# Query and key projections of the mLSTM heads: both halves of the input in one 512-column product, one bank per half unit

## The chip, the cores and the metric

The kernel runs on one core of a Trainium2 chip. The metric is device time in microseconds; the time of the kernel before is the median of three runs. The trace comes from one execution taken by the hardware profiler.

## The reference

Two layers of a hybrid decoder trunk on 256 tokens of width 1024. Each layer normalizes x, multiplies it by one input matrix whose columns are shared among three groups of heads (mLSTM, MoBA, NSA), lets each group mix the tokens, multiplies by an output matrix, and then runs a feed-forward block of width 4096. What the change touches is the mLSTM part of the input projection and the convolution behind it:

```python
h = rmsnorm(x, norm_mix[l])
proj = jnp.einsum('bsd,de->bse', h, w_in[l])
...
qk = jax.nn.silu(causal_conv(jnp.concatenate([m_q, m_k], axis=-1), conv_qk[l]))
...
y_m = mlstm(qk[..., :M_WIDTH], qk[..., M_WIDTH:], m_v, m_o, ...)
```

m_q and m_k are 512 columns each; causal_conv is a four-tap convolution along the tokens, each column with its own taps.

## The kernel before

All products are made with float32 operands split into two parts, a high one (the value cast to the fast format, `fp32r`) and a low one (the residue). A product of x and w is the sum of three: high x high, high x low, low x high. ScalarE casts each loaded weight piece (`raw`) to its high part (`hi`, in `highs`), VectorE subtracts to get the low part (`lo`, in `lows`), and six buffers hold each kind. The input, transposed, stands in one tile `H` of shape [128, 8, 2, 256]: for each of the eight blocks of 128 input columns, 256 tokens of the high part and beside them 256 tokens of the low part (`L.Hh`, `L.Hl`).

The input projection of a layer goes by the list `ORDER`: o1, o6, o2, o3, the compression products c0 and c1, q0, c2, c3, o4, q1, q2, q3, o5. The o groups are made by `project` with the tokens as output rows. The four q units are made by `project_t` with the projected columns as output rows: unit c2 covers 256 columns, as two halves c of 128, from two weight pieces of four blocks each. Before, both halves share one PSUM bank of the tag "acc", 2 x 256 columns; in each half and block the three products have 256 columns each and add into the same 256 columns.

PSUM has eight banks: "acc" is given two of them and "wk" six. Everything of the projections goes to "acc". A bank is given back by `free` when the step that reads it has been issued, and the next `new("acc", ...)` waits for that.

`conv` drains unit c2: one VectorE multiply with the row scales `RB` (line 1241) reads the whole bank into `cx`, behind three zero columns; then come the taps (a ScalarE multiply and three VectorE multiply-adds for each half), a tanh, and the write of `MQ`, which the mLSTM scores read (`mlstm`).

The order of instructions on each engine is fixed when the kernel is built. `Flow` (lines 145 to 279) runs all steps as generators with a rank, keeps an estimated clock of each engine from the costs in `Engine.cost`, and each time issues the operation that can start first; among operations of one engine that could start at about the same time the one with the lower rank goes first. `main` (the projections) has rank 100, the steps that prepare other operands have ranks from 2 up, and the casts and residues of weights (`highs`, `lows`) move ahead of these when their due time is near. On the chip each engine then works through its list in order and waits at the head of it.

Names in the trace: `acc` and `wk` are PSUM banks, `th`, `cx`, `cv` are buffers of SBUF, `P` holds attention scores after the exponential (ACT, `P<-wk,nmx`), `N` and `t` are the normalization and rotation of the attention heads, `KV` and `KC` belong to the compressed keys, `mr` to the mLSTM gates. All compute instructions carry the line of the helper, L137.

Of the kernel before, what the change touches and what calls it, by code (L numbers as in the profile page):

```python
# [11 lines left out]
ALU = mybir.AluOpType  # L12
# [3 lines left out]
S = 256  # L16
# [128 lines left out]
class Flow:  # L145
# [25 lines left out]
    def free(self, *tiles):  # L171
        for t in tiles:
            name = t.tensor.name
            self.places[self.owner.pop(name)].append(self.used.get(name, ("", 0.0))[1])
# [107 lines left out]
def body(ctx, tc, x, w_in, b_if, conv_qk, m_norm, moba_g, nsa_qg, nsa_kg, cmp_pe, cmp_w1, cmp_w2,  # L282
# [11 lines left out]
    done, free, add = flow.done, flow.free, flow.add  # L294
# [3 lines left out]
    mm, tr, act, copy = pe.matmul, pe.transpose, ac.activation, ac.copy  # L298
    tt, ts, stt = dv.tensor_tensor, dv.tensor_scalar, dv.scalar_tensor_tensor

    def new(tag, *shape, dt=F32):
        return New(tag, (128, *shape), dt)
# [89 lines left out]
    t = 0.0  # L392
    for l in range(DEPTH):
        for name in ORDER:
            if name[0] == "c":
                s = int(name[1])
# [83 lines left out]
    def weights():  # L480

        j = taken[0]
        taken[0] += 1
        yield f"lo {j}"
        if j >= SPLIT0:
            yield f"los {j}"
        _, kk, n = pieces[j]
        t = parts.pop(j)
        return tuple(a[:, :kk * n].rearrange("p (k n) -> p k n", k=kk) for a in t) + (t,)
# [80 lines left out]
    def project_t(l, c2):  # L570

        L = Ls[l]
        L.o[c2] = po = yield new("acc", 2, S)
        ws = []
        for c in range(2):
            for k in range(8):
                if len(ws) == k // 4:
                    ws.append((yield from weights()))
                wh, wl = (t[:, k % 4, c * 128:(c + 1) * 128] for t in ws[k // 4][:2])
                yield mm(po[:, c, :], wh, L.Hh[:, k, :], start=k == 0, stop=False)  # L580
                yield mm(po[:, c, :], wh, L.Hl[:, k, :], start=False, stop=False)
                yield mm(po[:, c, :], wl, L.Hh[:, k, :], start=False, stop=k == 7)
                if c and k % 4 == 3:
                    free(*ws[k // 4][2])
        done.add(f"q{c2}{l}")

    def compress(l, s):

# [128 lines left out]
    def main():  # L717
        for l in range(DEPTH):
            for name in ORDER:
                if name in ("c0", "c2"):  # L720
                    yield from compress(l, int(name[1]))
                elif name[0] == "c":
                    continue
                elif name[0] == "q":
                    yield from project_t(l, int(name[1]))
                else:
                    yield from project(l, name, GROUPS[name][1])
            yield from out_project(l)
            yield from feed_forward(l)
# [498 lines left out]
    def conv(l, c2):  # L1228
        L = Ls[l]
        yield f"RB{l}"  # L1230
        yield "V2"
        yield f"q{c2}{l}"
        if c2 == 0:
            L.MQt = yield new("MQ", 2048)
            L.MQ = L.MQt.rearrange("p (a b) -> p a b", a=8)
            done.add(f"MQ{l}")
        yield f"MQ{l}"
        xt = yield new("cx", 520)
        cx = xt.rearrange("p (a b) -> p a b", a=2)
        yield gp.memset(cx[:, :, 0:3], 0.0)  # L1240
        yield tt(cx[:, :, 3:259], L.o[c2], L.RB[:, None, :].to_broadcast([128, 2, S]), op=ALU.mult)
        free(L.o[c2])
        cv = yield new("cv", 2, 256)
        for c in range(2):
            w = lambda j: V[:, 32 + (l * 4 + j) * 8 + c2 * 2 + c:][:, 0:1]
            yield act(cv[:, c, :], cx[:, c, 0:256], AF.Copy, scale=w(0))
        for c in range(2):
            for j in range(1, 4):
                yield stt(cv[:, c, :], cx[:, c, j:j + 256], w(j), cv[:, c, :], op0=ALU.mult, op1=ALU.add)
        free(xt)  # L1250
        th = yield new("th", 2, 256)
        yield act(th, cv, AF.Tanh, scale=0.5)
        yield stt(L.MQ[:, 2 * c2:2 * c2 + 2, :], th, 1.0, cv, op0=ALU.add, op1=ALU.mult)
        free(th, cv)
        done.add(f"c{c2}{l}")
# [70 lines left out]
    for l in range(DEPTH):  # L1326
        gens = [after_mix(l, i, n) for i, n in tiles] + [after_ffn(l, i, n) for i, n in tiles]
        gens += [square_scales(l), scales(l), cmp_inputs(l)]
        gens += [nsa_heads(l, i) for i in range(2)] + [cmp_keys(l), gates(l)] + [moba_heads(l, i) for i in range(2)]
        gens += [attention(l, nsa), score(l, nsa), values(l), out_gates(l)] + [numerators(l, i) for i in range(2)]  # L1330
        gens += [mlstm(l)] + [conv(l, c) for c in range(4)] + [attention(l, moba), score(l, moba)]
        for g in gens:
            add(g, 2 + len(flow.procs))
# [36 lines left out]
```

## Time and profile before

| | us |
|---|---|
| median of three runs (641.97 to 692.95) | 642.06 |
| the profiled execution's own time | 641.33 |
| its span, first to last instruction | 639.5 |
| TensorE busy | 632.6 |
| VectorE busy | 444.3 |
| ScalarE busy | 367.1 |

The span is the stretch that the trace covers; the execution's own time is 1.8 us longer, and sums are made against that time. Matmuls are pipelined and their ends are modelled, so how fast TensorE gets on is read from the starts of two rows that follow each other. A row that ends in xN merges N instructions; its first number is the start of the first.

### The profile page before, as it was taken

The page shows a single profiled execution, that of the slowest core. Times are in us where ns is not written, and L with a number is a line of the kernel's source. Part 1 is how long each engine was busy: PE and PEld are TensorE (multiplying, and loading weights), DVE is VectorE, ACT ScalarE, POOL GpSimd, SP SyncE. Part 2 cuts the span into 40 slices and gives each one's busy share as a digit, 9 for nine tenths or more (in the row PEclk, how much of TensorE's full clock was granted, in tenths as well). Part 3 has the DMA queues.
Part 4 walks back from the last instruction along what each step waited for, and adds up shares of the span by engine and source line. Part 5 has one row for each costly group of instructions (what it writes and reads, how often), then busy time and mean ns, then how long its engine had stood idle before and what let it go on. Part 6 is the DMA issues. An engine that isn't in the chain of part 4 may idle for free.

```text
span 639.5 us, 10252 instructions
## 1 busy us (share of the span) xinstructions
PE 632.6 (99%) x3815; PEld 545.6 (85%) x3815; DVE 444.3 (69%) x823; ACT 367.1 (57%) x718; POOL 28.8 (4%) x50
## 2 busy tenths in 40 slices
PE   9999999999999999999999999999999999999997
PEld 8798898888888888888899979988888888888885
DVE  5769898679566565656583979987776565665661
ACT  6669875547364544545484985946645553545440
POOL 1110200100000000000010111001000000000000
PEclk9999999999999999999999999999999999999999
DMA  8787524448656465655546925144476656565711
GB/s 296 221 285 246 158 75 132 131 133 245 208 166 217 155 225 165 213 182 181 148 125 204 330 73 171 61 127 153 158 222 203 192 179 213 162 216 156 223 37 66
DMA packets 79090, 112.78 MB, mean 176 GB/s; under 512 B 4896, under 2 KB 61248, under 8 KB 79040
## 3 DMA queue, kind: packets, MB, share of 16 engines
q1 hardware_dynamic: 79008, 112.12, 55.5%
q8 instruction: 30, 0.49, 0.3%
q14 instruction: 20, 0.16, 0.1%
q10 hardware_dynamic: 32, 0.01, 0.0%
HBM read 111.06 MB, written 1.05 MB: 175 GB/s over the span
## 4 chain that ended last, share of the span: by engine, by line
PE 93%; DVE 2%; DMA 2%; ACT 1%; issue 0%; POOL 0%; DVEq 0%; POOLq 0%; ACTq 0%
PE wk L137 57%; PE acc L137 37%; DMA raw<-in_w_in 2%; DVE lo L137 1%; ACT hi L137 1%; DVE N L137 0%; POOL rs L137 0%; DVE t L137 0%; ACT P L137 0%; DVE dg L137 0%; ACT R L137 0%; DVE x L137 0%; ACT H L137 0%; DVE hss L137 0%; DVE nmx L137 0%
## 5 line engine op out<-in xcount | busy, mean ns | idle before, releaser
L137 DVE TENSOR_TENSOR lo<-raw,hi 128x1024 fp32r<-128x1024 f32 (+4 forms) x209 | 240.2, 1167 | 122.6 <-ACT hi L137 121.6
L137 ACT CAST hi<-raw 128x1024 fp32r<-128x1024 f32 (+3 forms) x207 | 205.7, 1014 | 133.5 <-PE wk L137 112.2
L137 PE MATMUL wk<-H,hi 128*128 128x512 f32 x512 | 128.0, 391 | 0.0
L137 PEld LDWEIGHTS wk<-H,hi 128*128 128x128 f32 x512 | 93.7, 188 | 17.9
L137 PE MATMUL acc<-hi,H 128*128 128x512 f32 (+3 forms) x368 | 100.1, 353 | 0.0
L137 PE MATMUL acc<-hi,P 128*128 128x512 f32 x240 | 79.2, 391 | 0.0
L137 PE MATMUL wk<-hi,P 128*128 128x512 f32 x240 | 78.7, 389 | 0.0
L137 PEld LDWEIGHTS wk<-H,lo 128*128 128x128 f32 x512 | 69.9, 190 | 5.0
L137 PE MATMUL wk<-H,lo 128*128 128x256 f32 x512 | 71.4, 282 | 0.0
L137 PEld LDWEIGHTS acc<-hi,H 128*128 128x128 f32 x368 | 63.9, 188 | 6.4 <-issue 0.4
L137 PE MATMUL acc<-lo,H 128*128 128x512 f32 (+3 forms) x184 | 65.2, 354 | 0.0
L137 PEld LDWEIGHTS wk<-hi,P 128*128 128x128 f32 x240 | 45.1, 188 | 9.3
L137 PEld LDWEIGHTS acc<-hi,P 128*128 128x128 f32 x240 | 45.2, 188 | 8.9
L137 PE MATMUL acc<-H,hi 128*128 128x256 f32 x256 | 51.3, 292 | 0.0
L137 PE MATMUL acc<-lo,P 128*128 128x512 f32 x120 | 47.0, 392 | 0.0
L137 PE MATMUL wk<-lo,P 128*128 128x512 f32 x120 | 46.7, 389 | 0.0
L137 ACT COPY th<-wk 128x256 f32<-128x256 f32 x64 | 23.9, 373 | 35.7 <-PE wk L137 35.7
L137 PEld LDWEIGHTS acc<-H,hi 128*128 128x128 f32 x256 | 40.4, 191 | 0.7 <-issue 0.5
L137 PEld LDWEIGHTS acc<-lo,H 128*128 128x128 f32 x184 | 34.6, 188 | 3.6 <-issue 0.7
L137 PE MATMUL acc<-H,lo 128*128 128x256 f32 x128 | 37.4, 292 | 0.1
L137 ACT ACTIVATE H<-wk,V 128x128 fp32r<-128x128 f32 x64 | 18.5, 373 | 22.7 <-PE wk L137 19.1
L137 DVE TENSOR_TENSOR cx<-wk,th 128x256 f32<-128x256 f32 x64 | 26.9, 421 | 2.2 <-ACT th L137 2.2
(199 smaller groups left out, 793.3 us busy)
## 6 DMA issues: line engine op xcount, KB each, us to landing
raw<-in_w_ff SPq DMA_DIRECT2D x128, 512.0 KB, 4.4
raw<-in_w_in SPq DMA_DIRECT2D x40, 512.0 KB, 5.1
raw<-in_w_out SPq DMA_DIRECT2D x16, 512.0 KB, 3.8
whole<-in_cmp_w SPq DMA_DIRECT2D x16, 256.0 KB, 4.8
raw<-in_w_in SPq DMA_DIRECT2D x8, 384.0 KB, 4.5
raw<-in_w_in SPq DMA_DIRECT2D x8, 268.0 KB, 3.5
raw<-in_w_in SPq DMA_DIRECT2D x8, 264.0 KB, 3.1
x<-in_x SPq DMA_DIRECT2D x4, 256.0 KB, 4.9
```

The costliest lines, as they stand in the source:

```text
L137: o = Op(self.name, lambda: f(out, *args, **kw), outs, ins, self.cost(op, outs, ins))
```

## The change

`project_t` now takes one bank of "acc" for each half of a unit. For each block the high weights multiply both parts of the input in one product of 512 columns, which leaves high x high in the bank's first 256 columns and high x low in the second 256. The low weights times the high input add 256 columns to the first half of the bank. Four wide products are followed by four narrow ones, for each of the two weight pieces. `conv` waits for each half by itself, copies the bank's second 256 columns to SBUF on ScalarE (into a `th` buffer), adds the first 256 columns on VectorE, and gives the bank back; the multiply with `RB` comes when both halves are in `cx`.

```diff
     def project_t(l, c2):
 
         L = Ls[l]
-        L.o[c2] = po = yield new("acc", 2, S)
         ws = []
+        g = dict(skip_group_check=True)
         for c in range(2):
-            for k in range(8):
-                if len(ws) == k // 4:
+            L.o[c2, c] = po = yield new("acc", 2, S)
+            for s in range(2):
+                if len(ws) == s:
                     ws.append((yield from weights()))
-                wh, wl = (t[:, k % 4, c * 128:(c + 1) * 128] for t in ws[k // 4][:2])
-                yield mm(po[:, c, :], wh, L.Hh[:, k, :], start=k == 0, stop=False)
-                yield mm(po[:, c, :], wh, L.Hl[:, k, :], start=False, stop=False)
-                yield mm(po[:, c, :], wl, L.Hh[:, k, :], start=False, stop=k == 7)
-                if c and k % 4 == 3:
-                    free(*ws[k // 4][2])
-        done.add(f"q{c2}{l}")
+                ks = range(s * 4, s * 4 + 4)
+                wh, wl = (t[:, :, c * 128:(c + 1) * 128] for t in ws[s][:2])
+                for k in ks:
+                    yield mm(po, wh[:, k % 4], L.H[:, k], start=k == 0, stop=k == 7, **g)
+                for k in ks:
+                    yield mm(po[:, 0, :], wl[:, k % 4], L.Hh[:, k, :], start=False, stop=k == 7, **g)
+                if c:
+                    free(*ws[s][2])
+            done.add(f"q{c2}{c}{l}")
...
-        yield f"q{c2}{l}"
+        yield f"q{c2}0{l}"
...
-        yield tt(cx[:, :, 3:259], L.o[c2], L.RB[:, None, :].to_broadcast([128, 2, S]), op=ALU.mult)
-        free(L.o[c2])
+        for c in range(2):
+            yield f"q{c2}{c}{l}"
+            o = L.o[c2, c]
+            t = yield new("th", 512)
+            yield copy(t[:, :S], o[:, 1, :])
+            yield tt(cx[:, c, 3:259], o[:, 0, :], t[:, :S], op=ALU.add)
+            free(o, t)
+        yield tt(cx[:, :, 3:259], cx[:, :, 3:259], L.RB[:, None, :].to_broadcast([128, 2, S]), op=ALU.mult)
```

The planner makes another order of it. The first place is TensorE in layer 0, where q0 ends and o4 begins. Before, acc_698 is q0's one bank and acc_883 is o4's; wk_681 is the compression, wk_900 the C,KV product.

```order
L137 MATMUL wk_849<-ident_79,cg_82 36x128 x2
L137 MATMUL acc_698<-H_70,hi_599 128x256 x2
L137 MATMUL acc_698<-H_70,lo_655 128x256
L137 MATMUL wk_681<-whole_699,MQ_439 32x128 x8
L137 MATMUL wk_681<-whole_715,MQ_439 32x128 x8
L137 MATMUL acc_883<-hi_641,H_70 128x512
L137 MATMUL acc_883<-lo_712,H_70 128x512
L137 MATMUL acc_883<-hi_641,H_70 128x512 x2
L137 MATMUL acc_883<-lo_712,H_70 128x512
L137 MATMUL wk_900<-C_85,KV_894 128x256
```

Now the same place, where acc_802 is the bank of q0's second half and acc_886, o4's, is the bank that q0's first half (acc_698) had.

```order
L137 MATMUL acc_802<-H_70,hi_599 128x512
L137 MATMUL acc_802<-H_70,lo_655 128x256 x4
L137 MATMUL wk_681<-whole_699,MQ_439 32x128 x8
L137 MATMUL wk_681<-whole_715,MQ_439 32x128 x8
L137 MATMUL wk_844<-ident_79,cg_82 36x128 x2
L137 MATMUL wk_873<-C_85,KV_862 128x256
L137 MATMUL acc_886<-hi_641,H_70 128x512
L137 MATMUL acc_886<-lo_712,H_70 128x512
```

The transposes of cg and the C,KV product now stand ahead of o4's first product, which takes a bank that q0 has just used. The second place is ScalarE's queue at the same time, in the new order; th_866 and th_885 are the copies of q0's two halves.

```order
L137 ACTIVATE P_799,sm01_771<-wk_752,nmx01_770 128x128
L137 ACTIVATE P_800,sm01_771<-wk_752,nmx01_770 128x128 x2
L137 ACTIVATE P_799,sm01_771<-wk_753,nmx01_770 128x128 x2
L137 COPY KV_862<-wk_681 128x128
L137 ACTIVATE P_800,sm01_771<-wk_753,nmx01_770 128x128 x2
L137 COPY th_866<-acc_698 128x256
L137 ACTIVATE KV_878<-wk_873 128x256
L137 COPY th_885<-acc_802 128x256
```

The copies stand behind the exponentials, and the reading of wk_873 stands between them. The third place is VectorE in layer 0, where q1 hands its first bank to q2. Before, q1's only read of its bank (acc_1095) stands here:

```order
L137 TENSOR_REDUCE nmx11_1235<-wk_1206 128x2
L137 TENSOR_REDUCE nmx11_1235<-wk_1207 128x2
L137 TENSOR_TENSOR Ml_72<-wk_897,Mh_71 128x2x128
L137 TENSOR_REDUCE nmx11_1235<-wk_1208 128x2
L137 TENSOR_REDUCE nmx11_1235<-wk_1209 128x2
L137 TENSOR_TENSOR cx_1257<-acc_1095,RB_97 128x2x256
L137 TENSOR_TENSOR lo_1215<-raw_996,hi_1198 128x1024
L137 TENSOR_TENSOR lo_1304<-raw_1051,hi_1258 128x1024
L137 RECIPROCAL sm11_1236<-sm11_1236 128x8
```

Now the bank of q1's first half is acc_1137, and its add is the last of these rows:

```order
L137 RECIPROCAL sm11_1088<-sm11_1088 128x8
L137 TENSOR_TENSOR N_1167<-R_708,hr81_1200 128x512
L137 TENSOR_TENSOR sm11_1088<-sm11_1088,GT1_102 128x4
L137 TENSOR_TENSOR N_1167<-N_1167,GB_91 128x256 x2
L137 TENSOR_SCALAR P_1151<-P_1151,sm11_1088 128x256
L137 TENSOR_TENSOR t11_728<-N_1167,C_85 128x128
L137 TENSOR_TENSOR t21_729<-N_1167,C_85 128x8x8 x2
L137 TENSOR_SCALAR P_1151<-P_1151,sm11_1088 128x256
L137 TENSOR_TENSOR N_1167<-t11_728,t21_729 128x8x16
L137 TENSOR_SCALAR P_1151<-P_1151,sm11_1088 128x256 x2
L137 TENSOR_REDUCE cnmx1_1243<-wk_1235 128x4
L137 TENSOR_TENSOR cx_1194<-acc_1137,th_1196 128x256
```

The read of q1's bank has moved from ahead of the reciprocal of the softmax sums to behind it, behind the norm of a head tile (N) and behind four scalings of P.

## Rows read from the trace of the kernel before

**Rows 1.** The page: busy time of each engine

```profile
PE 632.6 (99%) x3815; PEld 545.6 (85%) x3815; DVE 444.3 (69%) x823; ACT 367.1 (57%) x718; POOL 28.8 (4%) x50
```

**Rows 2.** The page: the chain that ended last, by engine

```profile
PE 93%; DVE 2%; DMA 2%; ACT 1%; issue 0%; POOL 0%; DVEq 0%; POOLq 0%; ACTq 0%
```

**Rows 3.** The page's groups: busy us, mean ns, idle before and what ended it

```profile
L137 DVE TENSOR_TENSOR lo<-raw,hi 128x1024 fp32r<-128x1024 f32 (+4 forms) x209 | 240.2, 1167 | 122.6 <-ACT hi L137 121.6
...
L137 PE MATMUL acc<-H,hi 128*128 128x256 f32 x256 | 51.3, 292 | 0.0
```

**Rows 4.** Timeline of TensorE, feed-forward of layer 0: start, us, instruction

```profile
145.24 1.98 PE L137 MATMUL wk<-H,hi 128*128 128x512 f32 x8
147.05 1.11 PE L137 MATMUL wk<-H,lo 128*128 128x256 f32 x8
148.01 0.64 PE L137 MATMUL wk<-H,hi 128*128 128x512 f32 x2
```

**Rows 5.** The tile th in the feed-forward stage: duration ns min/median/max

```profile
L137 ACT COPY th<-wk x64: 371/373/377, 153.8 to 619.5; 128x256 f32<-128x256 f32 x64
L137 DVE TENSOR_TENSOR cx<-wk,th x64: 416/418/426, 154.2 to 620.8; 128x256 f32<-128x256 f32 x64
```

**Rows 6.** Timeline of ScalarE in layer 0, the copy behind the exponentials

```profile
56.17 0.31 ACT L137 COPY KV<-wk 128x128 f32<-128x128 f32 x1
```

**Rows 7.** Timeline of TensorE in layer 0, o4's first products

```profile
55.53 0.50 PE L137 MATMUL acc<-hi,H 128*128 128x512 f32 x1
...
56.81 0.59 PE L137 MATMUL wk<-C,KV 128*128 128x256 f32 x2
57.05 0.82 PE L137 MATMUL acc<-hi,H 128*128 128x512 f32 x2
```

**Rows 8.** Timeline of ScalarE in layer 1, first instruction behind the exponentials

```profile
369.00 0.90 ACT L137 ACTIVATE cv<-cx,V 128x256 f32<-128x256 f32 x2
```

**Rows 9.** Timeline of TensorE in layer 1, o4's first products

```profile
368.09 0.50 PE L137 MATMUL acc<-hi,H 128*128 128x512 f32 x1
...
369.81 0.34 PE L137 MATMUL wk<-mr,SEL 128*128 128x384 f32 x1
```

**Rows 10.** Timeline of ScalarE in layer 0, from o4's end, and the large exponentials

```profile
72.17 1.05 ACT L137 CAST hi<-raw 128x1024 fp32r<-128x1024 f32 x1 [0.71 <-PE acc L137]
...
74.49 0.27 ACT L137 ACTIVATE Pc<-wk,cnmx 128x15 f32<-128x15 f32 x1
...
83.82 0.48 ACT L137 ACTIVATE P<-wk,nmx 128x256 f32<-128x256 f32 x1
...
87.91 0.96 ACT L137 ACTIVATE cv<-cx,V 128x256 f32<-128x256 f32 x2
```

**Rows 11.** Timeline of VectorE in layer 0, a head tile's norm; four scalings of P

```profile
78.51 0.69 DVE L137 TENSOR_TENSOR N<-R,hr 128x512 f32<-128x512 f32 x1 [0.65 <-POOL cx L137]
...
80.98 0.67 DVE L137 TENSOR_SCALAR P<-P,sm 128x128 f32<-128x128 f32 x3
...
93.80 1.13 DVE L137 TENSOR_SCALAR P<-P,sm 128x256 f32<-128x256 f32 x4
```

**Rows 12.** Timeline of TensorE in layer 0, scores with masks, and four transposes

```profile
75.75 0.71 PE L137 MATMUL wk<-QK 64*128 64x128 f32 x8
...
76.60 0.36 PE L137 MATMUL acc<-H,lo 128*128 128x256 f32 x1
...
84.08 0.60 PE L137 MATMUL wk<-ident,N 128*128 128x128 f32 x4
84.44 0.36 PE L137 MATMUL acc<-H,lo 128*128 128x256 f32 x1
```

**Rows 13.** Busy time by stretch: length, PE, PEld, DVE, ACT, POOL, PEclk, DMA, GB/s

```profile
72.00:103.00 31.00, 31.00 (x291) 29.03 (x290) 28.62 (x76) 23.99 (x75) 1.97 (x5) 1.00 0.28 86
...
634.00:636.00 2.00, 1.01 (x5) 0.51 (x3) 1.19 (x2) 0.00 (x0) 0.00 (x0) 1.00 0.33 129
...
637.00:640.00 3.00, 0.00 (x0) 0.00 (x0) 0.00 (x0) 0.00 (x0) 0.00 (x0) 0.63 0.13 49
```

## The prediction

> **What bounds the kernel now.** I read the page's busy shares first. TensorE is busy for 99% of the span, VectorE for 69%, ScalarE for 57% [rows 1]; the chain that ended last lies on TensorE for 93% of the span [rows 2]. So I look at how fast TensorE gets its products out and at what makes it wait, and other engines count only where it stands still for them. The groups by shape give the products that the change touches: 256 of 256 columns with the high weights [rows 3], and half as many with the low weights. Their pitch (from one start to the next) is read from the timeline, since the ends of matmuls are modelled. The feed-forward stage already runs both shapes of the new code: eight of 512 columns take 147.05 - 145.24 = 1.81 us, 0.227 each, and eight of 256 columns take 148.01 - 147.05 = 0.96 us, 0.120 each [rows 4]. Last I read the q stages themselves, TensorE's rows against those of ScalarE and VectorE, because that is where banks change hands.
>
> **The change part by part.**
> Products. A q unit of before issues 48 products of 256 columns, 48 x 0.120 = 5.76 us. Now it issues 16 of 512 and 16 of 256, 16 x 0.227 + 16 x 0.120 = 5.55 us. Each pair of 256 that becomes one 512 gives 0.240 - 0.227 = 0.013 us, and there are 128 pairs (the 256 high products of rows 3): 1.7 us of TensorE's own time. All of it lies on the path. What bounds this from the other side is 0, if the wide product came at twice the narrow pitch; 512 products of that shape in the feed-forward stage say it does not [rows 4], so I take 1.7.
> The Trainium skill ("TensorE: Matmul & The Clock Gate", section "Back-to-back issue gap") gives a product's pitch as its columns at 2.4 GHz plus about 2.5 ns. By it a merged pair would save only 2.5 ns, an estimate of 0.3 us over the 128. The rows show 13 ns, and the row decides.
>
> Banks. This is the costly part. "acc" has two banks. Before, a q unit holds one bank and gives it up after one VectorE multiply, so the next unit always finds the other bank free for 5.8 us. Now each half of a unit takes a whole bank. A half lasts 8 x 0.227 + 8 x 0.120 = 2.8 us, and the bank must be copied by ScalarE (0.37) and added by VectorE (0.42) [rows 5] before the half after next can start. There are 16 such hand-overs, eight a layer. Where the drain is slower than the other bank's 2.8 us, TensorE waits, and the order shows what the copy and the add now stand behind.
>
> q0 to o4, layer 0. o4's first product now needs the bank of q0's first half. Its copy stands on ScalarE behind all eight exponentials of the first attention tile. In before the last of them is over at 56.17 [rows 6]; one small copy now comes ahead of it, so about 56.3. Copy and add bring 57.1. Before, o4 began at 55.53 [rows 7]. The C,KV product, which the new order puts ahead of o4, fills 57.05 - 56.81 = 0.24 of that [rows 7]. Wait: 57.1 - 55.53 - 0.24 = 1.3 us. What is queued behind it on TensorE is all of o4, and behind the copy on ScalarE the activation for the compressed keys.
> q0 to o4, layer 1. The exponentials end at 369.00 [rows 8], copy and add bring 369.8; o4 began at 368.09, and 0.24 (C,KV) and 0.34 (one mr product) [rows 9] are pulled ahead of it: 1.1 us.
>
> q1 to q2, layer 0. q2's first product needs the bank of q1's first half. I count from the end of o4, which frees the buffer for ScalarE's last cast. ScalarE then has that cast, two reads of o4's bank and a square (72.17 to 74.49, 2.3 us), then a copy of QK and eight exponentials of 256 (83.82 to 87.91, 4.1 us) [rows 10]: 6.4. VectorE's reciprocal waits for the last exponential, and behind it stand the norm and rotation of the second MoBA head tile (78.51 to 80.98 is 2.5, of which about 0.4 is other work, so 2.1), four scalings of P (1.13) [rows 11], small ones (0.2), and then the add (0.42): 3.8. With two hand-offs between engines the bank is free about 10.3 us after o4. TensorE has for that time two halves (5.55), three groups of four transposes at 0.36 (84.08 to 84.44) [rows 12], one group of scores with masks at 0.85 (75.75 to 76.60) [rows 12] and about 0.5 of smaller products: 8.0. Wait: 2.3 us. Most of it is spent ahead of the transposes, which in the new order stand before q2 and need the same VectorE results.
> q1 to q2, layer 1. Here the norm comes before the last exponential. ScalarE needs 6.7, VectorE then 2.3, and TensorE has 8.2 us of work: 1.0 us.
>
> The other twelve. By the same count the bank comes free 0.1 to 4 us before TensorE arrives, so I find no wait for banks there. VectorE does two adds of 0.42 per unit more than before (the multiply stays, now from SBUF), 3.4 us a layer. That pushes two things back: in q3 of layer 0 the last scaled rows of P, which four transposes need, fall behind the multiply (0.8), and the scores of the last two mLSTM heads come about 0.3 to 0.6 late in each layer. I take 1.6 in all; the bounds are 0 and, if one residue of 1.17 us [rows 3] got ahead of each of four adds, about 5.
>
> The copies on ScalarE, 16 x 0.37 = 6 us, cost nothing by themselves: it has 43% idle [rows 1]. Without that cover they would cost their 6 us.
>
> Clock. The granted clock is 1.00, the 2.4 GHz level, in the q stages, as from 72 to 103 us [rows 13]. It leaves that level once in this trace, at the end: TensorE stops at 635.0 (busy 1.01 of the two us from 634), and from 637 to 640 the mean is 0.63 [rows 13], which puts the step to the 1.2 GHz level near 637.8, 2.8 us after the last product. The forecast's longest wait, 2.3 us, is shorter than that pause.
> The Trainium skill ("TensorE: Matmul & The Clock Gate", section "Part 1: The HAM clock gate") says that the throttled clock is the default, and that an engine which idles long enough is set back to it. The trace agrees at its end; whether a wait in the q stages is long enough no run here shows yet, and the sum by it is the third rival's.
>
> Sum, against the profiled execution's own 641.33 us (span 639.5 and 1.8 around it; the median of the runs is 642.06, 0.7 more): -1.7 + 1.3 + 1.1 + 2.3 + 1.0 + 1.6 = +5.6, so 646.9.
>
> **The rivals.**
> First, not slower: the banks come free in time, because copy and add, ready sooner than I count, run while TensorE still works on the products that the new order pulls ahead. Then 1.7 us is gained and the time is 639.6. For it: ScalarE and VectorE have room [rows 1]. Against it: o4's first product stands directly behind the drain in both layers, and the exponentials ahead of the copy have no reason to come sooner.
> Second, slower by over 2%: every hand-over is late, because a cast (1.05) [rows 10] and a residue (1.17) [rows 3] get ahead of copy and add each time. 1.05 + 1.17 + 0.37 + 0.42 is 3.0, only 0.2 over the 2.8 of cover. It decides from 0.9 us a hand-over, 16 x 0.9 - 1.7 = 12.7, so 654 and more. Against it: the order shows a cast or a residue there only in some places.
> Third, the clock: one or two waits last as long as the pause at the end and drop it to 1.2 GHz. Products then take twice their pitch for a while; at four or five us of that, some 2 to 2.5 us a fall, 649 to 652. For it: the wait in layer 0 is near the pause in the trace. Against it: it is broken by small products.
> Fourth, the change does not do what it says: the wide products cost as much as the pairs. Then the gain of 1.7 is missing, 648.7. The feed-forward rows speak against it.
>
> **How the numbers follow.** The forecast, 646.9, gets 0.72, and its own range is 643 to 651 (each of the five costs between half and one and a half of what I took). The first rival gets 0.13, the second 0.05, the third 0.07, the fourth 0.03. The range reaches from 640.0, most of the way to the first rival, to 653.0, which takes in the clock and leaves out the second. 2% of this time, 12.8 us, is about what a measurement of this kernel can tell from no change: faster by more than that 0.01, slower by more 0.05 (the second rival), within it 0.94.
>
> **What would show it.** In the new profile the rows of acc<-H,hi should be 128 of 512 columns at a pitch near 0.227. TensorE should stand still before o4's first product in both layers, released by VectorE's add into cx, for 1 to 1.5 us, and for 1 to 2.5 us in front of q2. The feed-forward and output stages should be as long as before. If o4 follows q0 without a gap, the bank part is wrong; if the granted clock falls below 1 inside the q stages, the third rival is right; if gaps stand before every half, the second.

## The result, and the profile after

The changed kernel took 647.23 us (median of 4 runs), the kernel before 642.01 beside it: a ratio of the fast runs of 1.0092, 95% interval 1.0073 to 1.0110. One run of the kernel before (692.95 us) was slow and is left out of that ratio. The change is slower by 0.9%, clear of no change but within 2%, and 0.3 us from the forecast of 646.9. The profiled execution took 647.17 us with a span of 645.4.

The page of the changed kernel: busy time, the granted clock in 40 slices, the chain that ended last, and two groups (busy us, mean ns, idle before).

```profile
PE 633.0 (98%) x3687; PEld 537.6 (83%) x3687; DVE 449.9 (70%) x839; ACT 372.3 (58%) x734; POOL 30.4 (5%) x50
...
PEclk9999989999999999999999999999999999999999
...
PE 84%; ACT 5%; DVE 4%; DMA 4%; SPq 1%; issue 1%; POOL 1%; ACTq 0%; DVEq 0%; POOLq 0%
...
L137 PE MATMUL acc<-hi,H 128*128 128x512 f32 (+3 forms) x368 | 99.7, 351 | 1.2 <-DVE cx L137 1.0
...
L137 PE MATMUL acc<-H,hi 128*128 128x512 f32 x128 | 40.5, 419 | 0.1
```

Against [rows 1 to 3]: 128 products of 512 columns stand where 256 of 256 did. TensorE's share of the last chain fell from 93% to 84%; ScalarE and VectorE, which empty the banks, now have 9% of it. The group acc<-hi,H, which begins o4, waits 1.0 us for cx. One slice of the granted clock (the row PEclk) shows an 8.

Where TensorE waited, by who released it (us in total, times, longest):

```profile
PE wk L137 <- DVE N L137: 3.4, 2, 1.9
...
PE acc L137 <- DVE cx L137: 1.0, 2, 0.8
PE wk L137 <- ACT KV L137: 0.9, 2, 0.6
```

These are the four places of the forecast, two in each layer: cx and KV stand in front of o4, N in front of q2. KV is the copy of the compressed keys and no bank; the forecast had only the bank there. TensorE's timeline shows them (start, us, instruction; in brackets the idle time before it and who ended it):

```profile
43.26 0.73 PE L137 MATMUL acc<-H,hi 128*128 128x512 f32 x2
...
54.30 0.39 PE L137 MATMUL wk<-ident,cg 128*36 128x128 f32 x2
55.05 0.70 PE L137 MATMUL wk<-C,KV 128*128 128x256 f32 x2 [0.35 <-ACT KV L137]
56.52 0.50 PE L137 MATMUL acc<-hi,H 128*128 128x512 f32 x1 [0.78 <-DVE cx L137]
...
80.24 1.08 PE L137 MATMUL acc<-H,hi 128*128 128x512 f32 x4
81.15 0.64 PE L137 MATMUL acc<-H,lo 128*128 128x256 f32 x4
81.63 1.09 PE L137 MATMUL acc<-H,hi 128*128 128x512 f32 x4
82.56 0.63 PE L137 MATMUL acc<-H,lo 128*128 128x256 f32 x4
...
85.54 0.78 PE L137 MATMUL wk<-ident,N 128*128 128x128 f32 x4 [1.95 <-DVE N L137]
86.12 1.06 PE L137 MATMUL wk<-ident,P 128*128 128x128 f32 x4
86.83 2.05 PE L137 MATMUL acc<-H,hi 128*128 128x512 f32 x4
88.81 1.35 PE L137 MATMUL wk<-QK 64*128 64x256 f32 x8
...
372.32 0.70 PE L137 MATMUL wk<-C,KV 128*128 128x256 f32 x2 [0.56 <-ACT KV L137]
...
373.64 0.50 PE L137 MATMUL acc<-hi,H 128*128 128x512 f32 x1 [0.17 <-DVE cx L137]
...
401.98 0.63 PE L137 MATMUL wk<-ident,N 128*128 128x128 f32 x4 [1.42 <-DVE N L137]
```

The first row is q0's start. By start-to-start distance over the usual one of the same product, o4 loses 0.50 + 1.04 = 1.54 us in layer 0 and 0.83 + 0.34 = 1.17 in layer 1, and the transposes of N in front of q2 come 2.10 and 1.58 late. What they wait for stands on ScalarE and VectorE, here in layer 0. First ScalarE's timeline:

```profile
55.20 0.41 ACT L137 ACTIVATE P<-wk,nmx 128x128 f32<-128x128 f32 x1
...
55.54 0.42 ACT L137 COPY th<-acc 128x256 f32<-128x256 f32 x1
...
66.51 0.49 ACT L137 ACTIVATE R<-acc,rs 128x256 f32<-128x256 f32 x1
...
82.44 0.43 ACT L137 COPY th<-acc 128x256 f32<-128x256 f32 x1
```

Then VectorE's:

```profile
56.05 0.42 DVE L137 TENSOR_TENSOR cx<-acc,th 128x256 f32<-128x256 f32 x1
...
85.12 0.28 DVE L137 TENSOR_TENSOR N<-t,t 128x128 f32<-128x128 f32 x1
...
85.97 0.41 DVE L137 TENSOR_TENSOR cx<-acc,th 128x256 f32<-128x256 f32 x1
```

The copy of q0's first half starts behind the eighth exponential of the tile (55.54), the add ends at 56.47, o4 begins at 56.52, so the bank sets the whole delay and the wait for KV lies inside it. In layer 1 the same add ends at 373.59 and o4 begins at 373.64. In front of q2 the bank is free at 86.4, 10.4 us after o4's end (75.98); 10.3 was forecast. TensorE's idle time there ends with N, whose transposes the new order puts ahead of q2; that the late bank is behind this order was argued from the order, and the runs below test it. In layer 1 q2 begins at 403.39, as the add that frees its bank ends (403.34). One thing was not in the forecast's sum, only among its rivals: the granted clock falls (windows: from and to, length, busy us of PE, PEld, DVE, ACT and POOL with their instructions, then the granted clock, the DMA share and GB/s).

```profile
84.00:85.00 1.00, 0.00 (x0) 0.00 (x0) 1.00 (x6) 1.00 (x3) 0.00 (x0) 1.00 0.86 348
85.00:86.00 1.00, 0.46 (x4) 0.49 (x5) 1.00 (x6) 1.00 (x2) 0.00 (x0) 0.94 0.08 33
86.00:87.00 1.00, 1.00 (x7) 1.00 (x6) 1.00 (x4) 0.98 (x4) 0.00 (x0) 0.50 0.00 0
...
89.00:90.00 1.00, 1.00 (x8) 0.70 (x8) 1.00 (x4) 0.00 (x0) 0.00 (x0) 0.85 0.78 307
```

TensorE stood still from 83.6 to 85.54; just after it had begun again, the clock went to 0.50, the 1.2 GHz level, for some 3.4 us. Four wide products took 88.81 - 86.83 = 1.98 us there, 0.92 at the 2.4 GHz level (82.56 - 81.63 is 0.93). Layer 1's wait of 1.42 us left the clock at 1.00.

To compare runs I use the **stretch** from a layer's first q product to its first feed-forward product, both starts read from TensorE's timeline. It leaves out the start of the program, which moves from trace to trace (q0 starts between 43.26 and 44.48), and the feed-forward stages. A stretch is read from one execution, and executions of one kernel differ by 1.3 to 4.7 us in time, so a difference of stretches under about 1 us is uncertain. The medians and ratios are from 4 to 12 executions, each set beside its own runs of the kernel before.

| kernel | layer 0 | layer 1 | sum | median us | ratio to before, 95% |
|---|---|---|---|---|---|
| before | 101.18 | 100.63 | 201.81 | 642.01 | |
| changed | 105.21 | 102.76 | 207.97 | 647.23 | 1.0092 [1.0073, 1.0110] |
| drain first | 101.63 | 101.05 | 202.68 | 643.01 | 1.0012 [0.9994, 1.0030] |
| drain behind due residues | 101.03 | 101.06 | 202.09 | 642.61 | 1.0019 [1.0009, 1.0028] |
| other bank | 100.43 | 101.59 | 202.02 | 641.34 | 0.9992 [0.9983, 1.0001] |
| drain first, q0 only | 100.62 | 99.85 | 200.47 | 640.26 | 0.9983 [0.9970, 0.9995] |
| drain first, q1 to q3 only | 103.48 | 100.91 | 204.39 | 644.13 | 1.0047 [1.0027, 1.0068] |
| three banks | 105.61 | 105.54 | 211.15 | 650.68 | 1.0124 [1.0105, 1.0143] |
| before with three banks | 107.40 | 105.73 | 213.13 | 651.83 | 1.0157 [1.0137, 1.0178] |
| narrow products | 105.86 | 101.54 | 207.40 | 647.52 | 1.0072 [1.0050, 1.0095] |
| drain first, narrow | 100.71 | 100.59 | 201.30 | 640.90 | 0.9994 [0.9984, 1.0003] |
| fillers in the wait | 104.77 | 104.00 | 208.77 | 648.30 | 1.0084 [1.0064, 1.0103] |
| drain, multiply on GpSimd | 99.85 | 101.62 | 201.47 | 640.24 | 0.9978 [0.9968, 0.9988] |
| multiply on GpSimd alone | 102.52 | 105.88 | 208.40 | 647.50 | 1.0083 [1.0061, 1.0104] |

The change costs 207.97 - 201.81 = 6.16 us in the stretch, 4.03 in layer 0 and 2.13 in layer 1. Outside of it the traced execution began q0 0.80 us earlier than that of the kernel before and lost 0.47 between the layers, which makes the 5.8 us by which it is longer.

### The profile page after: what moved, and what is told of

Same layout as the page of the kernel before. It is cut to its first block, busy times and chain, and to the rows that moved or that the text cites. A ratio compares the mean times of both kernels' runs of the same rounds, so it can differ in the third digit from the quotient of the medians.

```text
span 645.4 us, 10040 instructions
## 1 busy us (share of the span) xinstructions
PE 633.0 (98%) x3687; PEld 537.6 (83%) x3687; DVE 449.9 (70%) x839; ACT 372.3 (58%) x734; POOL 30.4 (5%) x50
## 4 chain that ended last, share of the span: by engine, by line
PE 84%; ACT 5%; DVE 4%; DMA 4%; SPq 1%; issue 1%; POOL 1%; ACTq 0%; DVEq 0%; POOLq 0%
PE wk L137 53%; PE acc L137 31%; DMA raw<-in_w_in 2%; ACT P L137 2%; DVE lo L137 1%; ACT hi L137 1%; DVE N L137 1%; ACT L137 1%; SPq L136 1%; DMA x<-in_x 1%; DMA GB<-in_nsa_q_norm 1%; ACT QK L137 1%; POOL hr L137 0%; DVE t L137 0%; DVE P L137 0%
## 5 line engine op out<-in xcount | busy, mean ns | idle before, releaser
L137 PE MATMUL acc<-H,hi 128*128 128x512 f32 x128 | 40.5, 419 | 0.1
L137 ACT ACTIVATE H<-wk,V 128x128 fp32r<-128x128 f32 x64 | 18.5, 370 | 22.0 <-PE wk L137 22.0
L137 ACT CAST P<-cv 128x512 fp32r<-128x512 f32 x30 | 18.6, 621 | 16.5 <-DVE cv L137 16.5
L137 PEld LDWEIGHTS wk<-lo,P 128*128 128x128 f32 x120 | 22.5, 188 | 4.7
```

Source lines behind the costliest of these rows:

```text
L137: o = Op(self.name, lambda: f(out, *args, **kw), outs, ins, self.cost(op, outs, ins))
```

## The experiments

My theory was the forecast's: the banks are emptied too late, because copy and add stand behind an attention tile's work. The rivals: the added work on ScalarE and VectorE itself costs the time; the wide products give nothing.

**Drain first.** Copy and add leave the convolution and become a step that is ready as soon as a half is done, with the most urgent rank.

```
+    def drain(l, c2, c):
...
+        yield copy(t[:, :S], o[:, 1, :])
+        yield tt(cx[:, c, 3:259], o[:, 0, :], t[:, :S], op=ALU.add)
+        free(o, t)
+        done.add(f"d{c2}{c}{l}")
...
             done.add(f"q{c2}{c}{l}")
+            add(drain(l, c2, c), 0)
```

> The changed kernel, but the copy and the add that empty a half's bank are a step of their own that the planner may place as soon as the half is done, ahead of the exponentials and norms it stood behind. Nothing is left out: the same copies, adds and products. Theory (the bank comes free too late, because its copy and add stand behind an attention tile's work): the waits in front of o4 and q2 shrink to a few tenths of a microsecond, the clock does not fall near 86 us, and of the 5.2 us by which the changed kernel is later than the one before most goes, leaving the gain of the products: 640 to 643. Rival (the copies and adds themselves, 16 of each, slow ScalarE and VectorE and so the whole stage): the work is the same, so it stays at 646 to 648.

643.01 us, at the theory's upper end; the stretch is 202.68, so 5.3 of the 6.2 us went with the same work on every engine (by the medians 4.3 of 5.2). Both waits for cx and for N are gone from the list of TensorE's waits, and the clock stays at 1.00. The rival falls. In place of those waits stand three others: 0.7 and 0.6 us for residues at 104 and 106, 0.9 for P at 419.

**Drain behind due residues.** The same with rank 1.6 in place of 0, which is behind a residue that is due (1.5).

> As the kernel with the drain as a step of its own, but that step now stands behind a weight residue that is due, and still ahead of attention. I count the stretch from the first q product to the first feed-forward product, both layers added, since what lies around it differs from run to run by up to a microsecond: 201.81 in the kernel before, 207.97 in the changed one, 202.68 with the drain first. Theory (the drain first lost some 2.2 us to waits for residues and for P that its copies and adds had pushed back, near 104, 106 and 419): those waits go and the stretch is 200 to 201.5, the time 640 to 642. Rival (VectorE is short of time there in any order): 202.5 or more.

202.09, between the theory's range and the rival's: only the start of layer 0 improved, and the time (642.61, ratio 1.0019) did not. The new waits stayed:

```profile
PE acc L137 <- DVE lo L137: 1.0, 2, 0.5
PE wk L137 <- DVE P L137: 0.7, 1, 0.7
```

So they do not come from the rank; the rival (VectorE short of time) is neither confirmed nor excluded.

**Another bank.** Copy and add stay inside the convolution; only the second half of each unit takes its bank from the six of "wk".

```
-            L.o[c2, c] = po = yield new("acc", 2, S)
+            L.o[c2, c] = po = yield new("wk" if c else "acc", 2, S)
```

> The changed kernel with its own order of copy and add, but the second half of each q unit takes its bank from the six that attention uses, not from the two of the projections. Theory (the wait is for the bank, not for the copy and add as such): o4 finds a bank of its own, so the wait for cx in front of it goes; attention has a bank less for some microseconds. Stretch 203 to 206 against 207.97 of the changed kernel, time 642 to 645. Rival (what comes late are the results of attention, whose work the copies push back): 207 to 208, as before.

641.34 us and 202.02, better than the theory's range: nearly all the cost goes with one line. TensorE's timeline in front of o4:

```profile
55.54 0.40 PE L137 MATMUL wk<-ident,cg 128*36 128x128 f32 x2
55.69 0.48 PE L137 MATMUL acc<-hi,H 128*128 128x512 f32 x1
```

o4 follows without a gap. It is the bank that is waited for, not the sum.

**Three banks, and the control.** `"acc": (pp, 3), "wk": (pp, 5)` in the changed kernel, then in the kernel before.

> The changed kernel with three banks for the projections and five for everything else, in place of two and six; nothing else is edited. Theory (what costs is that the half after next needs the bank of a half not yet emptied): with a third bank that half may wait 2.8 us longer, so the waits in front of o4 go and those in front of q2 shrink below 0.5 us: 641 to 643, if five banks are enough for the rest. Rival (copies and adds themselves): 646 to 648. If five banks are too few for the attention tiles, the time goes up instead, to 650 and more, and the kernel before with the same split will show how much of that is the five.

> The kernel before with three banks for the projections and five for the rest: the control for the changed kernel with that split. That one lost 3.6 us a layer at the start of the feed-forward stage, where transposes of x and Y waited (133 to 138 and 451 to 456), and was at 650.3. Theory (that loss is the five banks alone): it is here too, the stretch is 207 to 210 and the time 647 to 650, and so the third bank gave the changed kernel back all but 1 us of its hand-over waits. Rival (the loss comes from the change with three banks): the control stays at 642.

650.68 and 651.83 us. The waits in front of o4 and q2 went, but for 0.3 us for N (the stretch from q0 to o4 is 11.3 and 11.4 us, 11.47 and 10.77 in the kernel before), but five banks are too few at the entrance of the feed-forward stage. TensorE's waits there, in the changed kernel with three banks:

```profile
PE wk L137 <- DVE Y L137: 2.7, 2, 1.3
PE wk L137 <- DVE x L137: 2.2, 2, 1.1
PE wk L137 <- ACT Mh L137: 1.4, 2, 0.7
```

The control has the same three rows, with 1.3 in place of 1.4 in the last. The same loss stands in both; the control's stretch is above the theory's 207 to 210. The clock falls there in both as well (a mean of 0.85 from 136 to 140 us in the changed kernel, 0.64 there in the control). With equal banks the changed kernel is not slower than the other: 211.15 against 213.13. That supports the theory; how much of the 2 us is the products is not settled by it, since the falls differ.

**Narrow products.** Each product of 512 columns as two of 256 into the same bank, first in the changed kernel, then in the one with the drain first.

```
-                    yield mm(po, wh[:, k % 4], L.H[:, k], start=k == 0, stop=k == 7, **g)
+                    yield mm(po[:, 0, :], wh[:, k % 4], L.Hh[:, k, :], start=k == 0, stop=False, **g)
+                    yield mm(po[:, 1, :], wh[:, k % 4], L.Hl[:, k, :], start=False, stop=k == 7, **g)
```

> The changed kernel, but each product of 512 columns is written as two of 256 into the same two halves of the bank; banks, copies and adds stay. This prices the wide product alone. Theory (each merged pair gives 0.013 us, 128 pairs): 1.7 us longer than the changed kernel, 648.9, less what falls into waits that are there anyway, so 648.0 to 648.9. Rival (the wide product costs as much as the pair): 647.2, and 8 products of 512 take as long as 16 of 256.

> The kernel with the drain as a step of its own, with each product of 512 columns again written as two of 256. There TensorE hardly waits, so this prices the wide product better than the narrow version of the changed kernel, whose waits moved. Theory (0.013 us a pair, 128 pairs): the stretch is 1.7 us longer than 202.68, 204.4, and the time 643.5 to 645. Rival (wide products give nothing): 202.7.

Both missed: 207.40 and 201.30, 0.6 and 1.4 us shorter than with wide products, at 647.52 and 640.90 us. For the first the times don't tell the two apart (the intervals of the ratios overlap). The timeline of the second in layer 1:

```profile
401.16 1.12 PE L137 MATMUL acc<-H,hi 128*128 128x256 f32 x8
402.12 0.64 PE L137 MATMUL acc<-H,lo 128*128 128x256 f32 x4
```

Eight narrow products take 402.12 - 401.16 = 0.96 us; the four wide ones above take 81.15 - 80.24 = 0.91 and 82.56 - 81.63 = 0.93. So the wide product does give 0.04 us for four, 32 x 0.04 = 1.3 us over the kernel by the pitch, but the planner, which works with the cost of each product, made another order of each variant. With narrow products the three late waits of the drain-first kernel, 2.2 us, are not there, which outweighs the 1.3. A price of 0.010 us a pair can't be read from the total of two orders; it is read from the pitch, and no total here shows it.

The first of the two shows something on the clock, too. Its wait for N in layer 0 is 1.30 us, shorter than the changed kernel's, and the clock fell all the same (a row of TensorE's timeline, then a window):

```profile
85.74 0.63 PE L137 MATMUL wk<-ident,N 128*128 128x128 f32 x4 [1.30 <-DVE N L137]
...
88.00:90.00 2.00, 2.00 (x10) 1.18 (x10) 1.42 (x6) 1.90 (x8) 0.00 (x0) 0.50 0.26 55
```

**Fillers in the wait.** In layer 0, a step of the lowest rank issues small products into a bank that nobody reads, until q2 has its bank.

```
+    def keep_warm(l):
+        yield f"q11{l}"
+        wps = yield wk()
+        while f"b20{l}" not in done:
+            yield mm(wps[:, 0:128], idb, idb, start=True, stop=True)
+        free(wps)
```

> The changed kernel, with small products of 128 columns on data that nobody reads put between q1's end and q2's start in layer 0, so that TensorE does not stand still there; they add no result. This prices the fall of the clock (0.50 for 3.41 us from 85.89). Theory (the fall costs half of that stretch, about 1.5 us, beside the wait itself): the granted clock stays at 1.00 near 86 us and the time is 645.5 to 646.2. Rival (the fall costs nothing, as what comes after waits for VectorE anyway): clock 1.00 there, and 647.2. Second rival (the fillers are in the way of the transposes): 647.5 and more.

The clock stayed at 1.00, and the time was 648.30, not the theory's 645.5 to 646.2. TensorE's timeline:

```profile
84.77 2.92 PE L137 MATMUL wk<-B 128*128 128x32 bf16 x50
87.53 0.61 PE L137 MATMUL wk<-ident,N 128*128 128x128 f32 x4
...
88.39 1.17 PE L137 MATMUL acc<-H,hi 128*128 128x512 f32 x4
89.49 1.13 PE L137 MATMUL wk<-QK 64*128 64x256 f32 x8
```

The same place in windows (the granted clock is the third number from the end):

```profile
86.00:87.00 1.00, 1.00 (x22) 1.00 (x20) 1.00 (x5) 1.00 (x2) 0.00 (x0) 1.00 0.30 123
...
88.00:89.00 1.00, 1.00 (x10) 0.91 (x8) 1.00 (x3) 0.83 (x2) 0.00 (x0) 1.00 0.00 0
```

From the transposes of N to the scores it is 89.49 - 87.53 = 1.96 us here, 88.81 - 85.54 = 3.27 in the changed kernel: the fall costs 1.3 us up to there. But VectorE's timeline has N ready at 86.58 here, and its transposes begin at 87.53, behind fillers: the second rival was right as well. Layer 0 gained 0.44 net. Layer 1, which has no fillers but another order from there on, lost 1.24; that was not followed up. Its wait for N is 1.44 us, and the clock stayed:

```profile
403.63 0.63 PE L137 MATMUL wk<-ident,N 128*128 128x128 f32 x4 [1.44 <-DVE N L137]
...
404.00:406.00 2.00, 1.87 (x11) 1.10 (x11) 2.00 (x7) 1.63 (x7) 0.00 (x0) 1.00 0.00 0
```

**The multiply on GpSimd.** `gp.tensor_tensor` in place of `tt` for the sum times the row scale, 8 times; first with the drain of rank 1.6, then alone in the changed kernel.

> The kernel with all drains as steps of their own (behind due residues), with the multiply of the sum by the row scale moved from VectorE to GpSimd, since both its operands are in SBUF now: 8 x 0.69 us less on VectorE. Theory (with the drains first, what is left, waits of 0.5 to 0.7 us for residues and P near 103, 105 and 419, is VectorE's lack of time, 16 adds of 0.42 more than before): these waits go, the stretch is 199.5 to 201, 1 to 2 us under the kernel before, and the time 639.5 to 641. Rival (those waits come from where the planner puts residues, not from VectorE's load; or GpSimd's multiply is so slow that the convolution is late): 202 or more.

> The changed kernel with that multiply on GpSimd and nothing else edited. It takes more off VectorE (8 x 0.69 = 5.5 us) than the 16 adds of 0.42 less the cheaper multiply put on. Theory (the wait is for banks whose copy and add stand behind attention work in the order): it helps little, the stretch stays at 205.5 to 208, the time at 645 to 647.5. Rival (VectorE's added load is the cause): most of the 6.2 us goes, 201 to 203, and the time is 640.5 to 642.5.

With the drain: 640.24 us, as the theory said, and 201.47, which misses its 199.5 to 201. The waits for residues near 104 are gone (TensorE is busy for 7.00 of the 7 us from 100, for 5.98 without the multiply moved). That VectorE's load was what remained there does not follow: the kernel with the drain for q0 alone, further down, and the one with the drain first and narrow products keep the multiply on VectorE and are busy for 7.00 there too. So the load shows as a wait in one order and not in another, and load and order were not separated. The eight multiplies took 1.09 to 2.00 us on GpSimd, against 0.65 to 0.69 on VectorE in the changed kernel, and no row of TensorE's waits names it.

Alone: 647.50, the upper end of the theory's range. The wait in front of q2 moved within it: there is none in layer 0, and in layer 1 it is 1.44 us, after which the clock fell, though the same wait left it at 1.00 in the kernel with the fillers:

```profile
401.18 0.63 PE L137 MATMUL wk<-ident,N 128*128 128x128 f32 x4 [1.44 <-DVE N L137]
...
404.00:406.00 2.00, 2.00 (x13) 1.18 (x12) 0.86 (x4) 1.33 (x4) 1.06 (x2) 0.50 0.50 145
```

Layer 0 is 2.7 us shorter and layer 1 3.1 longer than in the changed kernel, the sum hardly moved. With the drain first, which leaves the load as it is and takes the cost away, this says that the load on VectorE is not the cause of the 6.2 us.

**One place at a time.** The drain as a step of its own for q0 alone, and then for q1 to q3 alone; the others keep the changed kernel's code.

```
-            add(drain(l, c2, c), 1.6)
+            c2 == 0 and add(drain(l, c2, c), 1.6)
```

> The changed kernel, with the drain as a step of its own (ranked behind weight residues that are due) for q0 alone; q1 to q3 keep the changed kernel's copy and add inside the convolution. This splits the 6.2 us of the stretch (201.81 before, 207.97 changed, 202.09 with all four drains first) between the two places. Theory (q0 to o4 costs 1.3 and 1.1, the rest is q1 to q2 and the clock): the stretch from q0 to o4 falls from 13.26 and 12.62 to about 11 in both layers, the one from q1 to o5 stays near 31.9 and 30.9, the sum is 204.5 to 206 and the time 644 to 646; near 86 us the clock falls as in the changed kernel. Rival (one delay runs on into the other, so that the first late drain is the cause of the second wait): 202 to 203.5.

> The counterpart of the kernel with the drain first for q0 alone: now q1 to q3 have it as a step of their own and q0 keeps the changed kernel's. That other kernel had a stretch of 200.47, so the drain of q0 alone took away 7.5 us, more than the two waits in front of o4 (1.54 and 1.17). Up to q1 TensorE's order is the changed kernel's here, so both waits in front of o4 should stay, the stretch from q0 to o4 near 13.2 and 12.6. Theory (a wait in front of o4 makes the planner put small products ahead of the end of o4's first tile, the MoBA queries come some 4 us later, and all of the second attention after it): the drain first in q1 takes away the wait for the bank, but the late attention stays and TensorE waits for it elsewhere: 205.5 to 208, time 645 to 647. Rival (the two places are independent, each with its own bank wait): the q1 to q2 part goes, 203.5 to 205.2, time 643 to 644.5.

q0 alone: 640.26 us, stretch 200.47, 7.5 less than the changed kernel though the two waits in front of o4 are only 1.54 + 1.17; my theory of separate prices missed, and the rival's side held, beyond its range of 202 to 203.5. ScalarE's timeline with the drain for q0 alone:

```profile
62.49 0.47 ACT L137 ACTIVATE R<-acc,rs 128x256 f32<-128x256 f32 x1 [0.17 <-PE acc L137]
...
80.56 0.44 ACT L137 COPY th<-acc 128x256 f32<-128x256 f32 x1
```

And TensorE's, at q0's start and in front of q2:

```profile
44.03 0.73 PE L137 MATMUL acc<-H,hi 128*128 128x512 f32 x2
...
83.09 0.63 PE L137 MATMUL wk<-ident,N 128*128 128x128 f32 x4 [0.32 <-DVE N L137]
```

R reads the end of o4's first tile, from which the MoBA queries are made. It comes 62.49 - 44.03 = 18.5 us after q0's start here and 66.51 - 43.26 = 23.3 in the changed kernel (20.1 in the kernel before). There the planner, which counts the wait in front of o4, had put small products (compressed keys, mr with its masks) ahead of the tile's last products. In the changed kernel the second attention is late with it, and so is the copy for q1 behind its exponentials: it starts 82.44 - 43.26 = 39.2 us after q0, 80.56 - 44.03 = 36.5 here. With q0 emptied in time, q1's unmoved copy is in time too: the wait for N is 0.32 and the clock stays.

q1 to q3 alone: 644.13 us, stretch 204.39. Here the other side held: R is as late as in the changed kernel (66.77, 23.0 after q0's start), both waits in front of o4 stand, yet the q1 to q2 part goes and attention is waited for nowhere else (what is new is mainly two waits for residues, 1.3 us in all). So the wait in front of q2 needs two things, a late attention tile and a copy behind it; taking away either removes it. And the drain of q1 to q3 is worth 3.6 us while q0 is late, but costs 202.09 - 200.47 = 1.6 once it is not, where the waits for residues and P near 104, 106 and 419 come with it.

The kernel with the drain for q0 alone and the one with the multiply on GpSimd beat both kernels, by 0.2% against the kernel before, far inside 2%: intervals [0.9970, 0.9995] and [0.9968, 0.9988]. Against the kernel before the first gains 1.34 us of stretch, about the products' 1.3; since the orders differ, that this is the products is not shown.

## Why the prediction was right, and where only its sum was

Direction and places were right, and so was the mechanism, a bank that is emptied behind an attention tile's work: TensorE stands still in front of o4 released by cx, in front of q2 released by N, in both layers, and the feed-forward stage is as long as before. That the second place stands by itself was wrong. The terms, forecast and measured:

| term | forecast | measured | from |
|---|---|---|---|
| wide products | -1.7 | -1.3 | pitch, 0.040 us for four |
| q0 to o4, layer 0 | +1.3 | +1.54 | start to start |
| q0 to o4, layer 1 | +1.1 | +1.17 | start to start |
| q1 to q2, layer 0 | +2.3 | +2.10 | start to start |
| q1 to q2, layer 1 | +1.0 | +1.58 | start to start |
| the clock | 0 | +1.3 | 3.27 - 1.96 |
| the other twelve, later VectorE work | +1.6 | -0.2 | what is left of 6.16 |

- **Products.** Mis-sized by 0.4. The step that took the pitch from eight wide products in a row [rows 4] overlooked that a half has only groups of four between narrow ones, where four take 0.92 instead of 4 x 0.227. In the section of the Trainium skill that the prediction cites, its formula is that of an isolated product, not of a stream in which every product loads its weights, which is what runs here; a merged pair gave 0.010 us.
- **q0 to o4.** Right by its own steps: copy behind eight exponentials, add, product. Its other result, that the order then changes, was not seen, and so the term was too small as a cause: emptying q0's bank in time is worth 7.5 us of the stretch, not 2.4.
- **q1 to q2.** The count from o4's end gave 10.3 us and was 10.4. Layer 1 was 0.6 too small. The step that treated it as a place of its own failed: the run with the drain for q0 alone removes it without touching it.
- **The clock.** "The forecast's longest wait, 2.3 us, is shorter than that pause" was the wrong step. The third rival came true once, at 1.3 us instead of 2 to 2.5; its four or five us at the lower level stood on no row, and the fall lasted 3.4. The pause after the last product [rows 13] is no lower bound for a pause between small products. The Trainium skill ("TensorE: Matmul & The Clock Gate", section "Part 1: The HAM clock gate") says that an engine which idles long enough is set back to the throttled clock. The traces agree that it can happen in the q stages, but the length of one wait does not decide it here: after 1.95 us, 1.30 us (narrow products) and 1.44 us (multiply on GpSimd alone) the clock went to 0.50, after 1.42 us and after 1.44 us (fillers, layer 1) it did not. What else decides is open.
- **The other twelve.** Forecast 1.6, measured about nothing, as what the other terms leave: the later VectorE work had room in the changed kernel. It became a wait (2.2 us) only in some of the kernels where the banks were free in time. So the near hit of the sum is luck: in the stretch it is 0.6 us off (6.16 against 5.6), with 1.3 us of clock, 0.6 of layer 1's second wait and 0.4 of products on one side and 1.8 of VectorE work that cost nothing on the other; that the time is only 0.3 off comes from the 0.80 us by which q0 happened to begin earlier, less the 0.47 between the layers.
- **Rivals.** The first (banks free in time, 639.6) is what the two best kernels show when the drain is placed for it: 640.26 and 640.24. The second (every hand-over late) did not occur; the fourth (wide products give nothing) is excluded by the pitch, not by any total.

## What to carry to other kernels

When a result is split over more banks, count when each bank is emptied and not only what emptying it costs: 16 copies and 16 adds cost nothing that shows in the kernel with the drain for q0 alone, their place behind exponentials cost 6 us, and another bank for one half, one line of the code, gave it back. Make the emptying of a bank a step of its own where the next user is close; for every unit, it pushed residues back in this order. In a planned program a wait at one place changes the order behind it, so the prices of two waits are not added before one has looked whether the second exists without the first.

## What the runs showed of the hardware

The granted clock fell to the 1.2 GHz level after TensorE stood still for 1.95 us (83.6 to 85.54), stayed there some 3.4 us, and products took twice their pitch (1.98 us for four, against 0.92); with small products in the gap it stayed at 1.00. A gap of 1.42 us left it at 1.00, as did one of 1.44 us in the kernel with the fillers, while gaps of 1.30 us (narrow products) and 1.44 us (multiply on GpSimd alone) were followed by 0.50: the same length went either way. At the end of the program of before it fell only 2.8 us after the last product [rows 13]. One multiply of 128x512 took 0.65 to 0.69 us on VectorE in the changed kernel, and on GpSimd 1.09 to 2.00 with the drain first and 1.09 to 3.13 without.
